# Linear attention with ReLU features: pairs of octets per load, six input buffers, K's copies in halves

## The chip, the cores and the metric

The kernel runs on one core of a Trainium2 chip. The metric is the device time of one execution in microseconds (us); a kernel's time is the median of several runs. A profile comes from one execution of its own.

## The reference

Q, K and V are fp32 arrays of 8 x 12 x 512 x 64 (batch, heads, sequence, dimension), drawn from a normal distribution.

```python
Q_feat = np.maximum(0, Q)
K_feat = np.maximum(0, K)
KV = np.einsum('bhkd,bhkv->bhdv', K_feat, V)
K_sum = np.sum(K_feat, axis=2)
numerator = np.einsum('bhqd,bhdv->bhqv', Q_feat, KV)
denominator = np.einsum('bhqd,bhd->bhq', Q_feat, K_sum)
return numerator / (denominator[:, :, :, None] + 1e-10)
```

Each of the 96 heads is independent. 36 MiB are read and 12 MiB written.

## The kernel before

**Tiling.** The 96 heads are taken in 12 octets of eight heads. An octet of one input is 1 MiB of fp32 that lies in one piece in memory; it is seen as 128 partitions of 8 KB (2048 numbers), so sixteen partitions hold one head. The loads are issued on POOL's queue (lines 176 to 187) and write bf16, 4 KB per partition, so the transfer casts. Only K and V of octet 0 are loaded otherwise: as fp32, from SP's queue, into two output buffers (line 264). There are seven buffers (`NI`) for each of Q, K and V, each a tile of its own, and ten output buffers of fp32 (`NOUT`).

**Waits and queues.** `Order` (line 9) works out which semaphores each instruction has to wait for, from the keys that instructions read and write; the program's order is written out by hand. Every load on POOL takes one of six lanes (semaphores gl0 to gl5) in turn and waits until the lane's load before it has landed, so at most six loads are under way. POOL issues its loads in program order: K, Q, V of octet 1, of octet 2 and so on. Before the first of them POOL clears and fills three small tiles: `ident` (line 268), the ones beside V in `vo` (lines 273 to 275) and `mask` (line 276).

**A step.** `step(i)` (line 311) does the first part of octet i and the last part of octet i - 1. PE transposes Q (line 363), ACT applies the ReLU (line 210), PE multiplies K by V in two halves of 16 products (line 372; half 0 waits for `a0` and `d0`, half 1 for `d1`), ACT copies the result out (line 218). Then the next octet is prepared: `prep_v` on ACT and DVE (lines 201 and 203), `copy_q` (line 207) and `prep_k` (line 192) on DVE. `prep_k` applies the ReLU and the mask and writes `kf`, once for each of two masks; for the octets of `HALVED` (2 to 8) each of the two copies is made in two halves, so that the first may start when PE has read half 0 of `kf`; for the others each is one instruction. DVE then normalises octet i - 1 (line 243, into `o_sb`), PE makes the denominators and the products with Q (line 357) and ACT copies these (line 226) for PE's transposes of the next step (line 381).

**Loads and stores in the steps.** Seven octets are loaded ahead of the steps; step i then loads octet i + 7, into the buffer of octet i. Stores go out on SP (line 252). Each store waits for its two normalised halves and, by a key that it reads, for K of the last octet to have landed: so no store moves before nearly all loads are through. In step 5, when all loads are issued, SP's program gets the stores of octets 0 to 3, then those of 4 and on.

Of the kernel before, what the change touches and what calls it, by code (L numbers as in the profile page):

```python
# [96 lines left out]
def kernel(  # L97
# [8 lines left out]
    B, H, S, D = Q.shape  # L106
    assert D == 64
    P = 128
    D1 = D + 1
    D4 = D + 4  # L110
    NH = B * H
    R = S * 4 // P
    RQ = S * 8 // P
    U = RQ // 2
    NO = NH // 8
    assert NO * 8 == NH and R == 16 and RQ == 32
    NI = 7
    NOUT = 10
    LANES = 6


    HALVED = range(2, 9)

    fp32 = mybir.dt.float32
    bf16 = mybir.dt.bfloat16
# [3 lines left out]
    sb = ctx.enter_context(tc.tile_pool(name="sb", bufs=1))  # L129
    psum = ctx.enter_context(tc.tile_pool(name="psum", bufs=1, space=bass.MemoryType.PSUM))  # L130

    def view(X, f):
        return X.rearrange("b h s d -> (b h s d)").rearrange("(n p f) -> n p f", p=P, f=f)

    Qr, Kr, Vr, Or = [view(X, RQ * D) for X in (Q, K, V, out)]

    ident = sb.tile([P, P], bf16, name="ident")
# [7 lines left out]
    q2 = sb.tile([P, U, P], bf16, name="q2")  # L145
# [2 lines left out]
    own = sb.tile([P, U, 8, 2], fp32, name="own")  # L148
    den = sb.tile([P, RQ], fp32, name="den")
    rec = sb.tile([P, RQ], fp32, name="rec")  # L150
    q_sb = [sb.tile([P, U, P], bf16, name=f"q_sb{i}") for i in range(NI)]
    k_sb = [sb.tile([P, RQ * D], bf16, name=f"k_sb{i}") for i in range(NI)]
    v_sb = [sb.tile([P, RQ * D], bf16, name=f"v_sb{i}") for i in range(NI)]
    o_sb = [sb.tile([P, RQ, D], fp32, name=f"o_sb{i}") for i in range(NOUT)]
    ps_kv = psum.tile([P, 2, 512], fp32, name="ps_kv")
    ps_den = ps_kv[:, 1, 256:512]
# [8 lines left out]
    def lane(who):  # L165
        turn[who] += 1
        return lanes[who][(turn[who] - 1) % len(lanes[who])]

    do = Order(nc, sems)

    def kv_src(o):
        if o == 0:
            return (o_sb[0], ("o", 0)), (o_sb[1], ("o", 1))
        return [(x[o % NI].rearrange("p (r d) -> p r d", d=D), (n, o % NI)) for n, x in (("k", k_sb), ("v", v_sb))]

    def load_q(o):
        do.op("pool", lambda e: e.dma_start(out=q_sb[o % NI].rearrange("p u f -> p (u f)"), in_=Qr[o],  # L177
                                            single_packet=True),
              writes=[("q", o % NI)], dma=lane("pool"))

    def load(o):
        i = o % NI
        for n, X, t in (("K", Kr, k_sb), ("V", Vr, v_sb)):
            if n == "V":
                load_q(o)
            do.op("pool", lambda e: e.dma_start(out=t[i], in_=X[o], single_packet=True), writes=[(n.lower(), i)],  # L186
                  dma=lane("pool"))

    def prep_k(o, s, halves=(0, 1)):
        src, key = kv_src(o)[0]  # L190
        rs = slice(R * halves[0], R * halves[-1] + R)
        do.op("dve", lambda e: e.tensor_scalar(kf[:, rs, s, :], src[:, rs], scalar1=0.0, scalar2=mask[:, 0, s:s + 1],  # L192
                                               op0=Alu.max, op1=Alu.mult),
              reads=[key, ("mask", 0)], writes=[("kf", s, j) for j in halves])
# [9 lines left out]
        do.op(who, make, reads=[key, ("mask", 1), "vo1"], writes=[("vo", t, j) for j in halves], sem=sem)  # L204

    def copy_q(o):
        do.op("dve", lambda e: e.tensor_copy(q2, q_sb[o % NI]), reads=[("q", o % NI)], writes=["q2"], sem="q2")  # L207

    def relu_q(j):
        do.op("act", lambda e: e.activation(qt[:, j * (U // 2):(j + 1) * (U // 2)], ps_qt[j], Act.Relu),  # L210
              reads=[("pq", j)], writes=[("qt", j)])
# [35 lines left out]
    def store(o):  # L247
        i = (o + 2) % NOUT
        to, src = Or[o], o_sb[i].rearrange("p r d -> p (r d)")
        keys = [("o", i, h) for h in range(2)]  # L250
        keys.append(("k", (NO - 1) % NI))
        do.op("sp", lambda e: e.dma_start(out=to, in_=src), reads=keys,
              dma=lane("sp" if o + NOUT < NO else "last"), kept=o + NOUT >= NO)
# [6 lines left out]
    def memset(who, ap, value, key):  # L260
        do.op(who, lambda e: e.memset(ap, value), writes=[key] if isinstance(key, (str, tuple)) else key)

    def body():
        for c, X in enumerate((Kr, Vr)):
            do.op("sp", lambda e: e.dma_start(out=o_sb[c].rearrange("p r d -> p (r d)"), in_=X[0]),  # L265
                  writes=[("o", c)], dma=lane("sp"))
        load_q(0)
        memset("pool", ident, 0.0, "ident")
        do.op("pool", lambda e: e.affine_select(out=ident, in_=ident, compare_op=Alu.not_equal, fill=1.0, base=0,
                                                pattern=[[-1, P]], channel_multiplier=1),  # L270
              reads=["ident"], writes=["ident"])
        ones = vo[:, :, :, 1:D4 - 1]
        memset("pool", ones[:, :, :, 0:D + 2:D1], 0.0, "vo1")
        for h in range(4):
            memset("pool", ones[32 * h:32 * h + 32, :, h % 2, 0:D + 2:D1], 1.0, "vo1")
        for h in range(4):
            for t in range(2):
                memset("pool", mask[32 * h:32 * h + 32, 1, t:t + 1], 1.0 if h % 2 == t else 0.0,
                       [("m", h, t), ("mask", 1)])
        for o in range(1, NI + 1):  # L280
            load(o)
            if o == 1:
                setup()
        for o in range(NO + 1):
            step(o)
        for n in lanes["pool"] + lanes["sp"]:
            nc.gpsimd.wait_ge(sems[n], do.count[n])
        nc.gpsimd.drain()

    def setup():  # L290
        do.op("dve", lambda e: e.tensor_copy(ident32, ident), reads=["ident"], writes=["ident32"])
        for c in range(2):
            do.op("dve", lambda e: e.tensor_reduce(
                out=mask_h[:, :, c], in_=ident32.rearrange("p (h b) -> p h b", h=8), op=Alu.add,
                axis=mybir.AxisListType.X), reads=["ident32"], writes=[("mh", c), "mask_h"])
        do.op("dve", lambda e: e.tensor_reduce(
            out=mask[:, 0, :], in_=mask_h[:, :, 0].rearrange("p (a s) -> p s a", s=2), op=Alu.add,
            axis=mybir.AxisListType.X), reads=["mask_h"], writes=[("mask", 0)])
        prep_k(0, 0)
        prep_k(0, 1)  # L300
        prep_v(0, 1, (0,), "act", "a0")
        prep_v(0, 0, (0, 1), "dve", "d0")
        prep_v(0, 1, (1,), "dve", "d1")
        do.op("dve", lambda e: e.memset(kvf.bitcast(fp32)[:, 0:4 * D1], 0.0), writes=KVD, sem="n0")
        do.op("dve", lambda e: e.memset(kvf.bitcast(fp32)[:, 4 * D1:], 0.0), writes=KVD, sem="n1")
        copy_q(0)
        for j in range(2):
            nc.scalar.sem_inc(sems[f"t{j}"], 1)
            do.note("act", "act", (), (), f"t{j}", 1)

    def step(i):
        r = i + 1
        more, last = i + 1 < NO, i == NO

        if not last:
            do.looped([("q2", r)], ["q2", "ident"], [("pq", 0)])
            do.looped([], ["q2", "ident"], [("pq", 1)])
            relu_q(0)
            relu_q(1)
            do.looped([("a0", r), ("d0", r)], KF[0], PK + ["pd"])  # L320
            do.looped([("d1", r)], KF[1], PK + ["pd"])
            evac_kv()
            if more:
                prep_v(i + 1, 1, (0,), "act", "a0")
                copy_q(i + 1)
                for halves in ((0,), (1,)) if i + 1 in HALVED else ((0, 1),):
                    prep_k(i + 1, 0, halves)
                    prep_k(i + 1, 1, halves)
        if i > 0:
            o = i - 1  # L330
            do.looped([("t0", r), ("t1", r)], [*OT, "ident32"], [("x", 0)])
            do.looped([], [*OT, "ident32"], [("x", 1)])
            for j in range(2):
                norm(o, j)
            if o + NI + 1 < NO:
                load(o + NI + 1)
            elif o + NI + 1 == NO:
                for x in range(o):
                    store(x)
            if o + NI + 1 >= NO:  # L340
                store(o)
        if not last:
            do.looped([("ev", r)], [*QT, *KVD], ["pd"])
            denominators()
            for j in range(2):
                do.looped([(f"n{j}", r)], [*QT, *KVD], [("x", j)])
            copy_ot(0, "act")
            copy_ot(1, "act" if more else "dve")
            if more:
                prep_v(i + 1, 0, (0, 1), "dve", "d0")  # L350
                prep_v(i + 1, 1, (1,), "dve", "d1")
# [48 lines left out]
    with tc.tile_critical(no_gpsimd_drain=True):  # L400
        body()
        products()
# [34 lines left out]
```

## Time and profile before

| | |
|---|---|
| median of 3 runs | 125.51 us (125.38 to 125.52) |
| profiled execution, its own time | 125.45 us |
| its span, first to last instruction | 123.7 us |
| PE, DVE, ACT, POOL busy | 69%, 69%, 63%, 20% |
| mean granted TensorE clock | 0.942 of full speed |
| read and written in HBM | 37.75 MB and 12.58 MB, 407 GB/s over the span |
| issues: loads on POOL, on SP; stores on SP | 34, 2; 12 |

The span is cut into 40 slices of 3.09 us in the page's table; a digit is the busy share of an engine in tenths. "DMA" is the share of the core's 16 DMA engines. A timeline line gives the start and the length in us, the engine, the line of the kernel, the operation, what it writes and reads, and in brackets the idle time before it and what ended it. A line on waits gives who waited for whom, the total in us, how often, and the longest. A line on one group's instructions gives least, median and largest duration in ns, then first and last start in us.

### The profile page before, as it was taken

The numbers are of one execution on the slowest core, as the hardware profiler recorded it, in microseconds if no ns is written. First come the engines' busy times: TensorE is split into PE (matmuls) and PEld (weight loads), VectorE is DVE, ScalarE is ACT, GpSimd is POOL, SyncE is SP. The second block draws the span as 40 slices with busy tenths as digits, with TensorE's granted clock in tenths as the row PEclk, the third lists the DMA queues.
The fourth block names the chain that finished last, engine by engine and source line by source line (L and its number), as shares of the span: only waits on it lengthen the run. The fifth ranks groups of instructions, "written<-read, shape, count | busy, mean of one in ns | idle before, by whom it ended". The sixth has DMA issues, their size and how long they took to land.

```text
span 123.7 us, 3418 instructions
## 1 busy us (share of the span) xinstructions
PE 85.0 (69%) x1440; PEld 73.7 (60%) x1440; DVE 84.9 (69%) x141; ACT 78.5 (63%) x108; POOL 24.9 (20%) x53
## 2 busy tenths in 40 slices
PE   0000098699797997979899797987969879655000
PEld 0000087699595986959689595876948759464000
DVE  1252921759989899898989989599595981937000
ACT  0000752996888989888998888889878888300000
POOL 5794111331131213212321131200000000000000
PEclk9999999859999999999999999999999999967855
DMA  2999999999999999999999999999999999999991
GB/s 58 391 315 236 212 215 217 216 212 213 213 213 212 212 213 212 212 216 215 212 212 215 220 212 212 215 215 212 212 307 423 424 427 427 424 429 432 427 427 42
DMA packets 6916, 32.55 MB, mean 263 GB/s; under 512 B 768, under 2 KB 768, under 8 KB 5120
## 3 DMA queue, kind: packets, MB, share of 16 engines
q0 software_dynamic: 4896, 17.83, 71.8%
q1 hardware_dynamic: 2016, 14.68, 28.7%
q14 instruction: 3, 0.02, 0.0%
q8 instruction: 1, 0.02, 0.0%
HBM read 37.75 MB, written 12.58 MB: 407 GB/s over the span
## 4 chain that ended last, share of the span: by engine, by line
PE 49%; DVE 30%; DMA 9%; issue 3%; ACT 1%; SPq 0%; DVEq 0%
DVE o_sb L243 22%; PE ps_kv L372 22%; PE ps_qt L363 11%; PE ps_x L381 10%; DMA o_sb<-in_V_dram 9%; PE ps_x L357 6%; DVE kf L192 3%; DVE vo L203 2%; ACT kvd L218 1%; DVE ot_sb L226 1%; PE ps_kv L357 0%; DVE q L207 0%; DVE den L235 0%; SPq L265 0%; DVE rec L238 0%
## 5 line engine op out<-in xcount | busy, mean ns | idle before, releaser
L243 DVE TENSOR_TENSOR o_sb<-ps_x,rec 128x1024 f32<-128x1024 f32 x24 | 28.5, 1220 | 6.5 <-PE ps_x L381 5.5
L372 PE MATMUL ps_kv<-vo,kf 64*128 64x132 bf16 x768 | 27.0, 230 | 0.6
L226 ACT COPY ot_sb<-ps_x 128x1024 f32<-128x1024 f32 x23 | 23.2, 1013 | 5.9 <-PE ps_x L357 4.9
L372 PEld LDWEIGHTS ps_kv<-vo,kf 64*128 64x128 bf16 x768 | 25.2, 100 | 2.4 <-issue 2.4
L381 PE MATMUL ps_x<-ident,ot_sb 128*128 128x128 f32 x192 | 25.2, 288 | 1.7 <-DVE ot_sb L226 1.7
L363 PE MATMUL ps_qt<-ident,q 128*128 128x128 bf16 x192 | 14.3, 234 | 16.8 <-DVE q L207 15.7
L192 DVE TENSOR_SCALAR kf<-k_sb,mask 128x1024 bf16<-128x1024 bf16 (+1 forms) x36 | 18.0, 542 | 9.9 <-PE ps_kv L372 9.5
L210 ACT ACTIVATE qt<-ps_qt 128x1024 bf16<-128x1024 bf16 x24 | 23.4, 1030 | 1.9 <-PE ps_qt L363 1.9
L381 PEld LDWEIGHTS ps_x<-ident,ot_sb 128*128 128x128 f32 x192 | 22.3, 148 | 3.2 <-issue 2.0
L363 PEld LDWEIGHTS ps_qt<-ident,q 128*128 128x128 bf16 x192 | 12.2, 106 | 19.5 <-DVE q L207 15.7
L218 ACT CAST kvd<-ps_kv 64x260 bf16<-64x260 f32 x48 | 18.0, 374 | 8.6 <-PE ps_kv L372 7.8
L357 PE MATMUL ps_x<-qt,kvd 128*128 128x256 bf16 x96 | 14.5, 275 | 7.3 <-DVE o_sb L243 7.0
L357 PEld LDWEIGHTS ps_x<-qt,kvd 128*128 128x128 bf16 x96 | 7.6, 98 | 12.0 <-DVE o_sb L243 10.5
L201 ACT ACTIVATE vo<-v_sb,mask 128x1024 bf16<-128x1024 bf16 x11 | 12.7, 1154 | 0.3
L203 DVE TENSOR_SCALAR vo<-v_sb,mask 128x2048 bf16<-128x2048 bf16 (+1 forms) x22 | 11.6, 569 | 0.0
L177 POOL DMA_DIRECT2D q_sb<-in_Q_dram x12 | 7.6, 630 | 18.2 <-DMA q_sb<-in_Q_dram 15.2
L186 POOL DMA_DIRECT2D v_sb<-in_V_dram x11 | 7.1, 650 | 18.3 <-DMA v_sb<-in_V_dram 17.0
L186 POOL DMA_DIRECT2D k_sb<-in_K_dram x11 | 6.8, 622 | 16.9 <-DMA k_sb<-in_K_dram 16.9
L207 DVE COPY q<-q_sb 128x2048 bf16<-128x2048 bf16 x12 | 8.2, 683 | 2.4 <-PE ps_qt L363 2.4
L201 ACT ACT_TABLE_LOAD x1 | 1.3, 1283 | 12.5 <-DMA o_sb<-in_V_dram 12.5
L357 PE MATMUL ps_kv<-kvd,qt 128*128 128x16 bf16 x192 | 6.9, 179 | 1.7 <-ACT kvd L218 1.7
L357 PEld LDWEIGHTS ps_kv<-kvd,qt 128*128 128x128 bf16 x192 | 6.5, 96 | 1.9 <-ACT kvd L218 1.8
(20 smaller groups left out, 26.5 us busy)
## 6 DMA issues: line engine op xcount, KB each, us to landing
out_dram<-o_sb SPq DMA_DIRECT2D x12, 1024.0 KB, 14.4
q_sb<-in_Q_dram POOLq DMA_DIRECT2D x12, 512.0 KB, 14.5
k_sb<-in_K_dram POOLq DMA_DIRECT2D x11, 512.0 KB, 14.4
v_sb<-in_V_dram POOLq DMA_DIRECT2D x11, 512.0 KB, 14.5
o_sb<-in_K_dram SPq DMA_DIRECT2D x1, 1024.0 KB, 6.5
o_sb<-in_V_dram SPq DMA_DIRECT2D x1, 1024.0 KB, 11.0
```

The lines of the kernel that those rows point to most:

```text
L186: do.op("pool", lambda e: e.dma_start(out=t[i], in_=X[o], single_packet=True), writes=[(n.lower(), i)], dma=lane("pool"))
L192: do.op("dve", lambda e: e.tensor_scalar(kf[:, rs, s, :], src[:, rs], scalar1=0.0, scalar2=mask[:, 0, s:s + 1], op0=Alu.max, op1=Alu.mult) ...
L201: make = lambda e: e.activation(to, src, Act.Copy, scale=m)
L203: make = lambda e: e.tensor_scalar(to, src, scalar1=m, scalar2=None, op0=Alu.mult)
L210: do.op("act", lambda e: e.activation(qt[:, j * (U // 2):(j + 1) * (U // 2)], ps_qt[j], Act.Relu), reads=[("pq", j)], writes=[("qt", j)])
L218: do.op("act", lambda e: e.copy(kvd[64 * c:64 * c + 64, s:8:2, c * D1:c * D1 + D1].rearrange("p (g t) d -> p g t d", t=2), ps_kv[64 * s:64 ...
L226: do.op(who, lambda e: e.copy(to, src) if who == "act" else e.tensor_copy(to, src), reads=[("x", j)], writes=[("ot", j)], sem=f"t{j}")
L243: do.op("dve", lambda e: e.tensor_tensor(o_sb[i][:, rs], ps_x[j].rearrange("p (r d) -> p r d", d=D), rec[:, rs].unsqueeze(2).to_broadcast( ...
L357: return pe.matmul(out_, lhsT, rhs, start=True, stop=True, skip_group_check=True)
L363: x = pe.transpose(ps_qt[u // 8][:, u % 8, :], q2[:, u, :], ident)
L372: x = pe.matmul(ps_kv[:, h, 0:2 * (D + 2)].rearrange("p (t d) -> p t d", t=2), kf[ps, R * g + k, :, :].rearrange("p s d -> p (s d)"), vo[p ...
L381: x = pe.transpose(ps_x[u // 8][:, u % 8 * P:u % 8 * P + P], ot[:, u].rearrange("p h c -> p (h c)"), ident32)
```

## The change

Three things are changed, and one at POOL's start.

- **Loads.** Octet 1 is loaded as before, K, Q, V, each for itself. From octet 2 on, the octets are loaded in pairs: one transfer for Q of both, one for K of both, then V of each. Octets 2 to 5 are loaded ahead of the steps; steps 1, 3 and 5 load the pairs 6/7, 8/9 and 10/11.
- **Buffers.** Six instead of seven for each input; the six lie side by side in one tile, so that a pair's transfer writes two neighbours.
- **K's copies.** `HALVED` is gone: `prep_k` is made in halves for all octets from 1 on.
- **POOL's start.** `ident` is cleared in four pieces of 32 columns; the ones' places in `vo` are cleared in four pieces of eight rows, and the ones are written in eight pieces, not four.

```diff
-    NI = 7
+    NI = 6
...
-    HALVED = range(2, 9)
...
-    q_sb = [sb.tile([P, U, P], bf16, name=f"q_sb{i}") for i in range(NI)]
-    k_sb = [sb.tile([P, RQ * D], bf16, name=f"k_sb{i}") for i in range(NI)]
-    v_sb = [sb.tile([P, RQ * D], bf16, name=f"v_sb{i}") for i in range(NI)]
+    ins = {n: sb.tile([P, NI, RQ * D], bf16, name=f"{n}_sb") for n in "qkv"}
...
-    def load(o):
-        i = o % NI
-        for n, X, t in (("K", Kr, k_sb), ("V", Vr, v_sb)):
-            if n == "V":
-                load_q(o)
-            do.op("pool", lambda e: e.dma_start(out=t[i], in_=X[o], single_packet=True), writes=[(n.lower(), i)],
-                  dma=lane("pool"))
+    def load(n, *octets):
+        o, i, m = octets[0], octets[0] % NI, len(octets)
+        src = {"q": Qr, "k": Kr, "v": Vr}[n][o:o + m].rearrange("n p f -> p n f")
+        do.op("pool", lambda e: e.dma_start(out=ins[n][:, i:i + m], in_=src, single_packet=True),
+              writes=[(n, x % NI) for x in octets], dma=lane("pool"))
+
+    def load_two(o):
+        load("q", o, o + 1)
+        load("k", o, o + 1)
+        load("v", o)
+        load("v", o + 1)
...
-        load_q(0)
-        memset("pool", ident, 0.0, "ident")
+        load("q", 0)
+        for c in range(4):
+            memset("pool", ident[:, 32 * c:32 * c + 32], 0.0, [("i", c), "ident"])
...
-        memset("pool", ones[:, :, :, 0:D + 2:D1], 0.0, "vo1")
+        for c in range(4):
+            memset("pool", ones[:, 8 * c:8 * c + 8, :, 0:D + 2:D1], 0.0, "vo1")
         for h in range(4):
-            memset("pool", ones[32 * h:32 * h + 32, :, h % 2, 0:D + 2:D1], 1.0, "vo1")
+            for j in range(2):
+                memset("pool", ones[32 * h:32 * h + 32, R * j:R * j + R, h % 2, 0:D + 2:D1], 1.0, "vo1")
...
-        for o in range(1, NI + 1):
-            load(o)
-            if o == 1:
-                setup()
+        for n in "kqv":
+            load(n, 1)
+        setup()
+        load_two(2)
+        load_two(4)
...
-                for halves in ((0,), (1,)) if i + 1 in HALVED else ((0, 1),):
-                    prep_k(i + 1, 0, halves)
-                    prep_k(i + 1, 1, halves)
+                for j in range(2):
+                    prep_k(i + 1, 0, (j,))
+                    prep_k(i + 1, 1, (j,))
...
-            if o + NI + 1 < NO:
-                load(o + NI + 1)
-            elif o + NI + 1 == NO:
-                for x in range(o):
-                    store(x)
-            if o + NI + 1 >= NO:
+            if i % 2 and i + 6 < NO:
+                load_two(i + 5)
+                if i + 7 == NO:
+                    for x in range(o):
+                        store(x)
+            if i + 7 >= NO:
                 store(o)
```

More of the change, by code (lines that the diff above doesn't have):

```diff
@@ L173, in kv_src @@
             return (o_sb[0], ("o", 0)), (o_sb[1], ("o", 1))
[L174 to L179, printed above, removed]
-    def load(o):
-        i = o % NI
-        for n, X, t in (("K", Kr, k_sb), ("V", Vr, v_sb)):
-            if n == "V":
-                load_q(o)
-            do.op("pool", lambda e: e.dma_start(out=t[i], in_=X[o], single_packet=True), writes=[(n.lower(), i)],
-                  dma=lane("pool"))
+        return [(ins[n][:, o % NI].rearrange("p (r d) -> p r d", d=D), (n, o % NI)) for n in "kv"]
+    def load(n, *octets):
[8 more added lines that the diff above has]
+        load("v", o + 1)
     def prep_k(o, s, halves=(0, 1)):
@@ L206, in copy_q @@
     def copy_q(o):
-        do.op("dve", lambda e: e.tensor_copy(q2, q_sb[o % NI]), reads=[("q", o % NI)], writes=["q2"], sem="q2")
+        do.op("dve", lambda e: e.tensor_copy(q2.rearrange("p u f -> p (u f)"), ins["q"][:, o % NI]),
+              reads=[("q", o % NI)], writes=["q2"], sem="q2")
     def relu_q(j):
```

## The prediction

> **What bounds the kernel now.** I read the 40 slices first, then the DMA queues, then what SP's queue and POOL waited for, then the timeline. The slices:
>
> ```profile
> DVE  1252921759989899898989989599595981937000
> DMA  2999999999999999999999999999999999999991
> GB/s 58 391 315 236 212 215 217 216 212 213 213 213 212 212 213 212 212 216 215 212 212 215 220 212 212 215 215 212 212 307 423 424 427 427 424 429 432 427 427 42
> ...
> q0 software_dynamic: 4896, 17.83, 71.8%
> q1 hardware_dynamic: 2016, 14.68, 28.7%
> ```
>
> The DMA engines are full from the second slice to the last but one, while DVE stops three slices (9 us) before the end. The loads look half as fast as the stores only because the row counts the bf16 that is written: 214 GB/s of it is 428 GB/s of fp32 read, the stores' rate. Now POOL's issues and SP's last wait:
>
> ```profile
> 29.28 0.53 POOL L186 DMA_DIRECT2D k_sb<-in_K_dram  x1 [1.93 <-DMA k_sb<-in_K_dram]
> ...
> 78.43 0.75 POOL L186 DMA_DIRECT2D v_sb<-in_V_dram  x1 [1.93 <-DMA v_sb<-in_V_dram]
> ...
> SPq L408 <- DMA out_dram<-o_sb: 7.5, 1, 7.5
> ```
>
> From the first of these issues to the second there are 20 steps: (78.43 - 29.28) / 20 = 2.4575 us per transfer of 1 MiB read. Each issue waits only for a lane (the transfer six before), so POOL follows the DMA and does not lead it. At the end SP waits 7.5 us for stores that were issued long before. The chain of waits names PE (49%) and DVE (30%), because it walks back from the last store's issue; but the last normalisation is over at 114.3 us and the span at 123.7:
>
> ```profile
> 113.08 1.23 DVE L243 TENSOR_TENSOR o_sb<-ps_x,rec 128x1024 f32<-128x1024 f32 x1 [0.35 <-PE ps_x L381]
> ...
> 120.00:121.00 1.00, 0.00 (x0) 0.00 (x0) 0.00 (x0) 0.00 (x0) 0.00 (x0) 0.50 0.76 320
> 121.00:122.00 1.00, 0.00 (x0) 0.00 (x0) 0.00 (x0) 0.00 (x0) 0.00 (x0) 0.50 0.14 57
> ```
>
> So the end is set by 48 MiB of transfers at 2.45 us each behind a start. The compute has slack: the last store moves for 2.45 us before its landing near 122.7 us, so its turn comes at 120.2; SP's first transfer was issued at 0.96 and moved data within about 1 us; it could be issued near 119 instead of 114.3, a **slack of some 4.7 us**. The two windows show one more thing: the DMA share falls to 0.14 before it is nil. One DMA engine runs behind the rest (landing records of the last store: 121.05 us on the first engine, 122.69 on the last; the same lag of 1.3 us is there from the load of K1 on). That late engine sets the end, and the others have over 1 us to spare.
>
> **Part 1, fewer transfers.** POOL issues 34 loads now (Q 12, K 11, V 11). After the change: Q0, three for octet 1, and per pair of octets Q, K, V, V, five times: 4 + 20 = 24, **ten fewer**, with the same bytes. What does one transfer cost beside its bytes? In the trace's packet records every transfer ends on each engine with one 4-byte packet of 22 ns (the page counts 768 packets under 512 B: 48 transfers by 16 engines), and data packets start 304.5 ns apart: 8 x 304.5 + 21.5 = 2457.5 ns, which is the whole pace above. So a removed transfer is worth 21.5 ns, ten of them **-0.21 us**, straight on the end, as the engines never idle. Bounds: nothing if those packets hide; at most what the best 1-us slice of the stores (437 GB/s, 2.40 us per MiB) leaves of the pace, 0.058 us, ten times: -0.58 us. I take -0.21, the measured packet.
>
> **Part 2, geometry of the pairs.** Each descriptor still reads 8 KB and writes 4 KB, but an engine now alternates between two octets 1 MiB apart. 20 MiB move so, 20 x 2.4575 = 49.15 us. The trace has no such transfer; nearest are today's loads and the stores, 2.4575 and about 2.45 us per MiB though one casts and the other doesn't, so I take no change. Each per cent of loss would be +0.49 us; a gain is bounded by Part 1's 437 GB/s, 20 x 0.058 = -1.2 us, and I see no reason for it.
> The Trainium skill (DMA: Bandwidth & Descriptors, Latency and other measured facts) reports that copies whose rows lie 512 KiB, 2 MiB or 4 MiB apart fall from about 214 to 207, 164 and 103 GB/s. No transfer of this trace has such rows; by its 2 MiB figure the sum would be 49.15 x (214/164 - 1), an estimate of 15 us more. Against it: here only two rows stand 1 MiB apart, and the 128 partitions lie side by side.
>
> **Part 3, the order of the loads.** Octet 1 keeps K, Q, V. After V1 (landed at 19.2 us) come Q of 2 and 3, K of 2 and 3, V2, V3: K2 lands after 4 MiB, 19.2 + 4 x 2.45 = 29.0 us (now 21.7), V2 at 31.4 (now 26.5). The users now:
>
> ```profile
> 27.74 1.83 DVE L192 TENSOR_SCALAR kf<-k_sb,mask 128x1024 bf16<-128x1024 bf16 x4 [1.14 <-PE ps_kv L372]
> ...
> 30.28 1.16 ACT L201 ACTIVATE vo<-v_sb,mask 128x1024 bf16<-128x1024 bf16 x1
> ```
>
> K2's copies start 29.0 - 27.7 = 1.2 us late, ACT's V copy 1.1 us late beside them. Queued behind on DVE: both normalisations of octet 0, so the n semaphores, PE's products and the ACT copies: the whole compute slips by 1.2 us. It doesn't grow: a pair of octets loads in 6 x 8 x 0.3045 + 4 x 0.0215 = 14.7 us, and two steps take 47.57 - 32.82 = 14.75 us (first Q transposes of steps 2 and 4), so later pairs arrive just as the slipped steps need them. V10 lands near 90.2 for an ACT copy now at 89.60, which the slip covers. All this lies in the 4.7 us of slack: **0**. Without that cover it would be +1.2 us.
>
> Lanes: a load still waits for the one six before it, and with doubles among these at least 7 MiB, 17 us of work, are in flight. Six buffers: the pair 6/7 overwrites octet 1's after step 0, which ends some 20 us before the lane frees at V2's landing or later. Stores: K of 10 and 11 is again followed by 2 MiB (V10, V11, before Q11, V11), so SP's twelve stores, gated on K11, go at the same place, 0.2 us earlier.
>
> **Part 4, K's copies in halves for octets 1, 9, 10, 11.** A step with whole copies is longer now: 77.09, 84.77, 92.58, 100.42 are the Q transposes of steps 8 to 11, periods 7.68, 7.81, 7.84 against 7.38: -0.30 - 0.43 - 0.46 = -1.2 us for compute, about what Part 3 costs it. DVE spends 1.83 instead of 1.42 us on four pieces, inside PE's product. Compute ends near 114.3 again; on the path: **0**. If loads didn't bound the end, both would count.
>
> **Part 5, POOL's start.** The clearing of ident goes from 1 to 4 pieces, vo's from 1 to 4, vo's ones from 4 to 8: ten more instructions ahead of K1's issue.
>
> ```profile
> L261 POOL MEMSET mask<- x8: 89/92/94, 5.0 to 6.0; 32x1 f32 x8
> L261 POOL MEMSET vo<- x5: 371/372/529, 2.7 to 4.5; 32x64 bf16 x4, 128x128 bf16 x1
> L261 POOL MEMSET ident<- x1: 224/224/224, 2.1 to 2.1; 128x128 bf16 x1
> ...
> 6.04 0.55 POOL L186 DMA_DIRECT2D k_sb<-in_K_dram  x1
> ...
> 7.63 1.38 POOL L186 DMA_DIRECT2D k_sb<-in_K_dram  x1
> 8.99 1.20 POOL L177 DMA_DIRECT2D q_sb<-in_Q_dram  x1
> ```
>
> One element costs 92 ns, and starts lie about 0.05 us further apart than durations. Ten more such floors are 10 x 0.14 = **+1.4 us** (0 if pieces only share the old time; if each cost its old whole, 3 x 0.27 + 3 x 0.58 + 4 x 0.42 = +4.2), so K1 is issued at 7.4 instead of 6.0 (10.3 at worst). There it meets DVE's fp32 copies of K0 (7.59 to 10.07), during which the two last rows took 1.38 and 1.20 us instead of 0.53: K1's issue ends near 8.8, and with SP's 1 us to first data it is ready at 9.8. The engines need it when K0, V0 and Q0, 3 MiB or 7.4 us from 2.7 on, are through: 10.1, and 11.3 on the late engine. **0**, with 1.5 us to spare where it counts.
> The Trainium skill (SBUF — State Buffer, Who interferes with whom) says why those rows are long: a tensor_scalar copy in a 2-port mode holds the ports that GpSimd shares, and the other side blocks fully. The trace agrees: 1.38 against 0.53.
>
> **Sum**: 125.45 (profiled execution; span 123.7 and 1.75 around it) - 0.21 = 125.24. The median of the runs is 0.06 higher than that execution, so **125.3**. About 0.2% (0.25 us) is what a measurement here can tell from no change; the forecast lies just inside it.
>
> **Rivals.**
> *K1 comes too late* (slower). Place: the start, Part 5. It decides once K1 is ready later than 11.3 us on the late engine, that is memsets dearer by over 2.9 us in place of 1.4. At worst: issued 10.3, done 10.8, data 11.8, hence +0.5 on the late engine, -0.21: 125.8; with a second slow issue behind it 126.0. For: ten more floors, DVE's hold. Against: the small instructions are cheap by their rows. 0.13.
> *Pairs move slower* (slower). Part 2 at 1%: +0.49 - 0.21 = 125.8; slower than before by 0.2% from 0.9% on. For: never seen here. Against: two different kinds of transfer keep one pace. 0.08. The row-pitch rule of the Trainium skill, cited under Part 2, speaks for this rival.
> *Compute becomes the bound.* It needs a slip over 4.7 us where 1.2 - 1.2 is expected; a slip repeated in each of the five pairs would be 6.0 - 1.2 = 4.8, +0.1 - 0.21 at most: 125.3 to 125.4, and 125.9 if each slip were 1.3. 0.04.
> *It saves nothing*, the small packets being covered, or a small loss eating the gain: 125.5. For: 22 ns is close to what two packets overlap (324 long, 304.5 apart). 0.12.
> *More is saved*: Part 1's upper bound, 124.9. Against: the packet records leave no other gap. 0.05.
>
> **How the numbers follow.** The forecast has 0.58, with its own range 125.0 to 125.45; 0.36 of it lies under 125.26. Faster 0.36 + 0.05 = 0.41; within 0.2% 0.22 + 0.12 = 0.34; slower 0.13 + 0.08 + 0.04 = 0.25. The range, 124.9 to 126.0, goes from Part 1's upper bound to the late K1.
>
> **What would show it.** Right: 608 packets under 512 B instead of 768; the DMA row full as before; POOL's K1 issue near 7.4 us; DVE's K copy of octet 2 waiting for a DMA until about 29.0; last normalisation near 114.3, SP's last wait about 7.3 us. Wrong: a DMA slice under 9 near 10 us (K1), load slices below 210 GB/s (pairs), or SP's last wait gone (compute).

## The result, and the profile after

The changed kernel takes 126.15 us in the median of 13 runs (125.62 to 126.95). The kernel before, run beside it, takes 125.39 (125.24 to 125.72, 13 runs). The ratio is 1.006, with a 95% interval of 1.0038 to 1.0082: **slower by 0.6%**. The forecast was 125.3, and the range ended at 126.0. The profiled execution of after took 125.79 us, 0.34 more than that of before; its span is 124.0 against 123.7. This profile thus shows less than half of the loss of 0.76 us between the medians; longer runs of after are profiled under the experiments. All ratios here are of fast runs; the only slow ones are four of the twelve of `e13_less_late`, its profiled run among them.

The slices of after's page:

```profile
DVE  0354725624976989989898998989899895596100
...
PEclk9999999999559999999999999999999999999755
DMA  2999999999999999999999999999999999999991
GB/s 61 403 311 217 201 209 217 211 215 214 214 214 211 211 217 215 211 215 217 213 215 211 214 215 214 213 215 214 215 312 422 420 426 428 423 426 431 434 412 42
DMA packets 6756, 32.55 MB, mean 263 GB/s; under 512 B 608, under 2 KB 608, under 8 KB 4960
```

The small packets are 608, as ten transfers fewer should make them. From the seventh slice to the last load the rate is that of before. Only slices 4, 5 and 6 are lower: 217, 201, 209 where before had 236, 212, 215. The DMA row hides it: it shows a 9 in those slices too. POOL's start in after's timeline (start, length, engine, line, operation):

```profile
2.12 0.69 POOL L256 MEMSET ident<- 128x32 bf16 x4
...
3.12 3.29 POOL L256 MEMSET vo<- 128x32 bf16 x12
6.46 1.13 POOL L256 MEMSET mask<- 32x1 f32 x8
7.54 1.32 POOL L174 DMA_DIRECT2D k_sb<-in_K_dram  x1
8.85 1.20 POOL L174 DMA_DIRECT2D q_sb<-in_Q_dram  x1
10.04 0.54 POOL L174 DMA_DIRECT2D v_sb<-in_V_dram  x1
```

K1 is issued at 7.54 us, where before issued it at 6.04. The fills of `vo` now take 3.29 us instead of 2.25, those of `ident` 0.69 instead of 0.22. What the DMA engines did in two of the next microseconds; the last three columns are clock, DMA share and GB/s. After:

```profile
10.00:11.00 1.00, 0.00 (x0) 0.00 (x0) 0.00 (x0) 0.00 (x0) 1.00 (x3) 1.00 0.97 160
...
13.00:14.00 1.00, 0.00 (x0) 0.00 (x0) 1.00 (x3) 0.99 (x2) 0.20 (x1) 1.00 0.93 188
```

And before:

```profile
10.00:11.00 1.00, 0.00 (x0) 0.00 (x0) 0.07 (x1) 0.00 (x0) 0.19 (x1) 1.00 1.06 217
...
13.00:14.00 1.00, 0.00 (x0) 0.00 (x0) 1.00 (x2) 0.99 (x2) 0.00 (x0) 1.00 1.16 233
```

When K0, V0 and Q0 are through, the engines find too little queued: 160 GB/s instead of 217, and 188 instead of 233 three microseconds later. At 214 GB/s the first is (217 - 160) / 214 = 0.27 us of work lost, and the second, against a steady 214, (214 - 188) / 214 = 0.12 us: together 0.39 us. The packet records show it too: between 8 and 20 us before has no data packet that takes over 0.5 us, while after has ten, of 0.54 to 0.69 us, all starting between 10.12 and 10.48 us. They lie on the loads' queue and are probably the first of K1; the records do not name the transfer.

The landing records have 16 times for each transfer, one for each DMA engine. The span ends 0.99 us behind the last of them, before and after. They give a balance for the late engine, which sets the end:

| us | before | after | difference |
|---|---|---|---|
| V of octet 1 landed | 19.16 | 19.64 | +0.48 |
| from there to V of octet 11 landed | 75.07 | 74.86 | -0.21 |
| from there to the last store landed | 28.46 | 28.48 | +0.02 |
| last store landed | 122.69 | 122.98 | +0.29 |

So, in this profile, **the loss is all made before 20 us**, and the ten saved transfers are there, at the predicted size, between. The lag of the late engine differs from run to run; the mean of the 16 landings is steadier. V of octet 1 landed at 18.04 us in the mean before and at 18.40 after, +0.36, close to the 0.39 of the two windows; from there to the last store the mean takes 103.37 us before and 103.22 after, -0.15. The compute is later too; three lines of after's timeline, and what SP waited for at the end:

```profile
29.58 1.74 DVE L186 TENSOR_SCALAR kf<-k_sb,mask 128x1024 bf16<-128x1024 bf16 x4 [3.92 <-DMA k_sb<-in_K_dram]
...
31.95 1.16 ACT L195 ACTIVATE vo<-v_sb,mask 128x1024 bf16<-128x1024 bf16 x1 [3.40 <-DMA v_sb<-in_V_dram]
...
112.75 2.36 DVE L238 TENSOR_TENSOR o_sb<-ps_x,rec 128x1024 f32<-128x1024 f32 x2 [1.32 <-PE ps_x L380]
```

```profile
SPq L407 <- DMA out_dram<-o_sb: 7.0, 1, 7.0
```

DVE waits 3.92 us for K2 (the two 5s of the clock row are behind this wait), and the last normalisation ends at 115.1 instead of 114.3. SP still waits 7.0 us after that for stores, so these 0.8 us cost nothing.

### The profile page after: what moved, and what is told of

The parts are those of the page before. It is cut to its first block, busy times and chain, and to the rows that moved or that the text cites. A ratio compares the mean times of both kernels' runs of the same rounds, so it can differ in the third digit from the quotient of the medians.

```text
span 124.0 us, 3416 instructions
## 1 busy us (share of the span) xinstructions
PE 84.2 (68%) x1440; PEld 72.5 (58%) x1440; DVE 86.2 (70%) x149; ACT 78.3 (63%) x108; POOL 22.1 (18%) x53
## 3 DMA queue, kind: packets, MB, share of 16 engines
q0 software_dynamic: 4736, 17.83, 71.7%
## 4 chain that ended last, share of the span: by engine, by line
PE 43%; DVE 24%; DMA 15%; POOL 7%; issue 4%; POOLq 0%; DVEq 0%; SPq 0%
DVE o_sb L238 21%; PE ps_kv L371 17%; DMA k_sb<-in_K_dram 15%; PE ps_x L380 11%; PE ps_qt L362 9%; PE ps_x L356 5%; POOL vo L256 2%; POOL q_sb L174 2%; DVE kf L186 1%; POOL k_sb L174 1%; DVE ot_sb L221 1%; PE ps_kv L356 1%; POOL mask L256 1%; POOL v_sb L174 0%; POOL ident L256 0%
## 5 line engine op out<-in xcount | busy, mean ns | idle before, releaser
L186 DVE TENSOR_SCALAR kf<-k_sb,mask 128x1024 bf16<-128x1024 bf16 x44 | 19.4, 485 | 9.8 <-PE ps_kv L371 5.3
L380 PE MATMUL ps_x<-ident,ot_sb 128*128 128x128 f32 x192 | 23.6, 276 | 1.7 <-DVE ot_sb L221 1.7
L380 PEld LDWEIGHTS ps_x<-ident,ot_sb 128*128 128x128 f32 x192 | 20.8, 140 | 3.2 <-issue 2.0
L356 PE MATMUL ps_x<-qt,kvd 128*128 128x256 bf16 x96 | 15.3, 287 | 9.2 <-DVE o_sb L238 8.8
L195 ACT ACTIVATE vo<-v_sb,mask 128x1024 bf16<-128x1024 bf16 x11 | 12.7, 1154 | 3.6 <-DMA v_sb<-in_V_dram 3.4
L174 POOL DMA_DIRECT2D q_sb<-in_Q_dram x7 | 5.4, 771 | 9.1 <-DMA v_sb<-in_V_dram 5.8
L174 POOL DMA_DIRECT2D k_sb<-in_K_dram x6 | 4.9, 821 | 6.8 <-DMA v_sb<-in_V_dram 5.1
```

Of the source, the lines that this page charges most:

```text
L174: do.op("pool", lambda e: e.dma_start(out=ins[n][:, i:i + m], in_=src, single_packet=True), writes=[(n, x % NI) for x in octets], dma=lane ...
L195: make = lambda e: e.activation(to, src, Act.Copy, scale=m)
L356: return pe.matmul(out_, lhsT, rhs, start=True, stop=True, skip_group_check=True)
L380: x = pe.transpose(ps_x[u // 8][:, u % 8 * P:u % 8 * P + P], ot[:, u].rearrange("p h c -> p (h c)"), ident32)
```

## The experiments

Theory: POOL's longer start issues octet 1's loads late, and the engines run short of work near 10 us. Rivals: the pairs themselves are slower; DVE's fp32 copies of K0, which share the time from 7.5 to 10 us with the issues, hold them up; the compute sets the end in the longer runs; the way in which the fills are split does the harm, not the time they take. Where an expectation uses a short name, A2 is the theory of DVE's copies, F the fetch of code that the first runs brought up, and G a fixed time of 3 to 4 us from POOL's issue to data. All the kernels compute the whole reference. The runs at a glance, each ratio against the kernel before on the same chip:

| run | K1 issued at | GB/s, 10 to 11 us | median us | ratio, 95% interval |
|---|---|---|---|---|
| e1_old_fills | 6.02 | 217 | 125.82 | 1.0023 (1.0013 to 1.0033) |
| e2_new_fills_alone | 7.55 | 152 | 125.99 | 1.0045 (1.0027 to 1.0063) |
| e3_loads_first | 2.10 | 213 | 125.46 | 0.9997 (0.9989 to 1.0006) |
| e4_after_again | 7.54 | 180 | 126.53 | 1.0068 (1.0046 to 1.0090) |
| e5_pad_after | 6.02 | 221 | 125.35 | 0.9996 (0.9987 to 1.0004) |
| e6_before_loads_first | 2.12 | 217 | 125.39 | 1.0001 (0.9992 to 1.0009) |
| e8_pad_ahead | 6.47 | 217 | 125.33 | 0.9991 (0.9982 to 0.9999) |
| e9_late_by_pads | 7.69 | 148 | 125.97 | 1.0049 (1.0029 to 1.0070) |
| e10_k1_first | 2.12; Q1 at 10.11 | 225 | 126.28 | 1.0070 (1.0051 to 1.0088) |
| e11_k0_on_act | 7.55 | 107 | 125.90 | 1.0045 (1.0027 to 1.0063) |
| e12_later_still | 11.46 | 41 | 128.75 | 1.0275 (1.0254 to 1.0297) |
| e13_less_late (spoiled) | 6.84 | 205 | 126.21 | 1.0051 (1.0027 to 1.0075) |
| e14_octets_2_3_single | 7.54 | 148 | 125.72 | 1.0026 (1.0014 to 1.0037) |
| e16_pad_and_single | 6.48 | 225 | 125.47 | 0.9996 (0.9987 to 1.0004) |
| e18_less_late_clean | 6.85 | 217 | 125.44 | 0.9998 (0.9989 to 1.0007) |
| e19_early_k0_on_act | 6.48 | 209 | 125.37 | 0.9994 (0.9985 to 1.0004) |

**The fills alone, and the loads alone.** `e1_old_fills` is after with POOL's old fills; `e2_new_fills_alone` is before with the new ones. Both differ from their base by these lines:

```diff
-        for c in range(4):
-            memset("pool", ident[:, 32 * c:32 * c + 32], 0.0, [("i", c), "ident"])
+        memset("pool", ident, 0.0, "ident")
...
-        for c in range(4):
-            memset("pool", ones[:, 8 * c:8 * c + 8, :, 0:D + 2:D1], 0.0, "vo1")
+        memset("pool", ones[:, :, :, 0:D + 2:D1], 0.0, "vo1")
         for h in range(4):
-            for j in range(2):
-                memset("pool", ones[32 * h:32 * h + 32, R * j:R * j + R, h % 2, 0:D + 2:D1], 1.0, "vo1")
+            memset("pool", ones[32 * h:32 * h + 32, :, h % 2, 0:D + 2:D1], 1.0, "vo1")
```

> The changed kernel with POOL's fills of ident and vo in the old few pieces, so that K1 of octet 1 is issued near 6.0 us again; pairs, six buffers and halves stay. Theory A (K1, and with it Q1, is issued too late, the DMA engines run dry near 10 us): the loss goes and the saved packets show, 125.2 us, ratio to before 0.998, little spread. Theory B (transfers of two octets are slower): as the changed kernel, about 126.1. Theory C (the compute, held up by the later K2, becomes the bound in the longer runs): about 126.1 with its spread of over 1 us.

> The kernel before with the new fills alone (ten more instructions on POOL ahead of K1); loads, buffers and copies as before. Theory A: slower by the whole loss, 0.76 plus the 0.21 that the pairs save, some 126.3 us, with the wide spread of the changed kernel. Theories B and C: 125.4, as before.

e2, with no pair in it, is slower by 0.45%, at 125.99 us where the theory asked for 126.3: the fills alone bring a loss, and the same low window:

```profile
10.00:11.00 1.00, 0.00 (x0) 0.00 (x0) 0.02 (x1) 0.00 (x0) 1.00 (x3) 1.00 0.89 152
```

e1 has K1 at 6.02 us and no low window, and yet it was 0.2% slower than before, where 0.2% faster was expected. Its last store landed at 122.66 us, no later than before's 122.69, but its span is 124.1. What lies behind the last store is a small transfer in the last microsecond:

```profile
121.00:122.00 1.00, 0.00 (x0) 0.00 (x0) 0.00 (x0) 0.00 (x0) 0.00 (x0) 0.50 0.10 41
122.00:123.00 1.00, 0.00 (x0) 0.00 (x0) 0.00 (x0) 0.00 (x0) 0.00 (x0) 0.50 0.00 0
123.00:124.00 1.00, 0.00 (x0) 0.00 (x0) 0.00 (x0) 0.00 (x0) 0.00 (x0) 0.50 0.03 8
```

The packet records name it: 8 KB on q14, the queue of instructions, at 123.997 us. In after the last such packet comes at 72.5 us, in before at 79.4. e1's POOL program is ten instructions shorter than either of these: before has ten more loads, after ten more fills.

**The same loads, issued early.** `e3_loads_first` keeps the new fills and puts octet 1's loads ahead of them; `e4_after_again` is after itself in the same batch.

```diff
         load("q", 0)
+        for n in "kqv":
+            load(n, 1)
         for c in range(4):
...
-        for n in "kqv":
-            load(n, 1)
         setup()
```

> The changed kernel with K, Q and V of octet 1 issued right behind Q of octet 0, ahead of all fills, which keep their new pieces. Theory A: no dry engines at 10 us, 125.2 us, faster than before by 0.2%. Theories B and C: about 126.1.

> The changed kernel once more on this chip, for a second profile and its spread beside the others: about 126.1 us, runs from 125.6 to 127. Theory A: in a longer run the DMA share between 10 and 18 us is lower and the landing of V1 later by what the run is longer. Theory C: V1 lands as in the first profile, and SP's last wait for the stores is gone.

e3 has no low window:

```profile
10.00:11.00 1.00, 0.00 (x0) 0.00 (x0) 0.05 (x1) 0.00 (x0) 0.63 (x7) 1.00 1.04 213
```

It takes 125.46 against 126.53 for after beside it: **moving three issues takes the whole loss away**, with all the pairs and all the fills still there. V1 lands at 18.99. The expected gain of 0.2% did not come: the kernel is as fast as before.

**The length of the program.** `e5_pad_after` is e1 with ten tiny fills of a spare tile behind the loads that are issued ahead of the steps; `e8_pad_ahead` has them ahead of K1. `e6_before_loads_first` is before with octet 1's loads ahead of the fills.

```diff
+    spare = sb.tile([P, 16], fp32, name="spare")
...
+        for c in range(10):
+            memset("pool", spare[0:32, c:c + 1], 0.0, ("spare", c))
```

> The run with the old fills, and ten tiny fills of a spare tile on POOL behind its ahead-of-time loads (near 30 us, where POOL waits anyway), so that POOL's program is as long as the changed kernel's. In the run with the old fills the last landing was at 122.66 us, yet an 8 KB code fetch began at 123.997 and the span ended at 124.1. Theory F (its 0.33 us over the kernel before is that code fetch behind the last wait, which a longer program moves forward): no fetch after 120 us, 125.45. Theory B (the transfers of two octets cost it): 125.8 as without the ten.

> The same ten tiny fills with the old fills, but ahead of K1's issue, which they move from 6.0 to about 7.4 us, as in the changed kernel; program as long as there. Theory A (only the lateness counts, not what POOL does meanwhile): 126.2 with a spread of over 0.7 us, DMA rate between 10 and 11 us down to 150 to 180 GB/s from 217. Else, if the split fills themselves cost it: 125.5.

> The kernel before (single octets, seven buffers, old fills) with K, Q, V of octet 1 issued ahead of the fills, the counterpart of the changed kernel with its loads first (125.46). Theory A as it stands (the engines never run dry here, before or after): 125.45, as before. If the pairs cost time that the early issue hides in their run: 125.2 here.

e5 is back at 125.35, with no packet of code behind 72.7 us. Ten useless instructions made e1 faster by 125.82 - 125.35 = 0.47 us between the medians. In the profiles the span ends 1.41 us behind the last store's landing in e1 and 0.99 us in e5, as in before and after: 0.42 us of it is the fetch. e8 missed its expectation: ten such fills, which wait for nothing, cost only 0.39 us together, so K1 was hardly late:

```profile
6.13 0.39 POOL L257 MEMSET spare<- 32x1 f32 x10
6.47 0.55 POOL L175 DMA_DIRECT2D k_sb<-in_K_dram  x1
```

So e8 is one more kernel with pairs and early loads, at 125.33. e6 shows that loads earlier than before's 6.04 us bring nothing.

**Late by other means.** `e9_late_by_pads` has the old fills and ten dearer ones ahead of K1, each of which waits for the one before; `e12_later_still` has twenty. In `e10_k1_first` only K1 goes ahead of the new fills, Q1 and V1 stay behind. In `e11_k0_on_act` ACT makes the two copies of K0, so DVE is idle while POOL issues.

```diff
+    spare = sb.tile([P, 16], bf16, name="spare")
...
+        for c in range(10):
+            memset("pool", spare, 0.0, ["spare", ("mask", 1)])
         for n in "kqv":
             load(n, 1)
```

```diff
-        prep_k(0, 0)
-        prep_k(0, 1)
+        for s in range(2):
+            src, key = kv_src(0)[0]
+            do.op("act", lambda e: e.activation(kf[:, :, s, :], src, Act.Relu, scale=mask[:, 0, s:s + 1]),
+                  reads=[key, ("mask", 0)], writes=[("kf", s, j) for j in range(2)])
```

> Old fills, and ahead of K1's issue ten dearer fills of a spare tile (16 columns, each waiting for the one before), which move the issue to about 7.5 us; the ten tiny ones of the run before had moved it to 6.47 only, at no loss. Theory A (lateness alone): 126.2 with a wide spread, a dip of the DMA rate at 10 to 11 us. If the split fills themselves are the cause: 125.35.

> The changed kernel with K1 alone issued ahead of the fills, Q1 and V1 where they were. Theory A in its narrow form (the engines run dry once, when Q0 and V0 are through and K1 is not there): 125.5. If the second dip of the changed kernel near 13 us (188 and 156 GB/s in its two profiles) is a lateness of Q1 by itself: 125.8 to 126.0, with that dip and without the one at 10 us.

> The changed kernel, with the two copies of K0 made on ACT in place of DVE (ACT waits for V0 at that time anyway): K1 is still issued at 7.5 us, but DVE makes no fp32 copy beside it. Theory A1 (the issue alone is late): K1's packets still miss 10.1 us by little, 125.8 or more. Theory A2 (the issue is late and meets DVE's copies, which stretch POOL's issues and what stands behind them): issues of 0.55 us in place of 1.3 and 1.2, V1 out by 9.2 us, no dips, 125.35.

> As the run with ten dear fills ahead of K1, with twenty: K1 is issued at about 9.3 us instead of 7.69. Where the DMA rate came back in the late runs, K1's data flowed 3.1 to 3.9 us behind the start of its issue. Theory G (from POOL's issue to data 3 to 4 us at this place, whatever DVE does): data flow again at 12.4 to 13.2 us, the late engine loses 1.1 to 1.9 us: 126.4 to 127.2. Theory A as first priced (issue 1.3 us and 1 us to data): data at 11.6, a loss of 0.3 on the late engine, 125.6 to 125.8.

e9, whose fills are the old ones, is as slow as e2: the time counts, not the way the fills are split. In e10 the eight fills of `mask`, which fell beside DVE's copies of K0, took 3.17 us instead of 1.13, and Q1 was issued at 10.11. The loss, 0.7% at 126.28 us, is larger than the 125.8 to 126.0 that was expected, and the low windows moved with the late issue:

```profile
12.00:13.00 1.00, 0.00 (x0) 0.00 (x0) 0.51 (x1) 0.53 (x1) 1.00 (x2) 1.00 0.87 172
13.00:14.00 1.00, 0.00 (x0) 0.00 (x0) 1.00 (x2) 0.99 (x2) 0.90 (x1) 1.00 0.79 156
```

In e12 the twenty fills, among which the same copies fell, took 5.41 us, so K1 was not issued at 9.3 us as expected, but at 11.46:

```profile
6.12 5.41 POOL L257 MEMSET spare<- 128x16 bf16 x20
11.46 0.55 POOL L175 DMA_DIRECT2D k_sb<-in_K_dram  x1
```

```profile
11.00:12.00 1.00, 0.00 (x0) 0.00 (x0) 0.00 (x0) 0.00 (x0) 0.83 (x5) 1.00 0.04 16
12.00:13.00 1.00, 0.00 (x0) 0.00 (x0) 0.81 (x1) 0.83 (x1) 1.00 (x3) 1.00 0.60 41
13.00:14.00 1.00, 0.00 (x0) 0.00 (x0) 1.00 (x2) 0.99 (x2) 1.00 (x2) 1.00 0.60 98
```

Here the engines stand idle, which measures what the prediction had to borrow from SP: the ten first packets of K1 that the records have were taken up at 12.7 to 12.8 us, took 0.6 to 1.1 us each, and data flowed at the usual 0.32 us a packet from 13.7. That is **2.2 us from the start of POOL's issue and 1.7 from its end**, not 1.0, and, with idle engines, not the 3 to 4 us that one theory held. The run took 128.75 us, more than either theory had expected, as the issue came two microseconds later than planned.

In e11 DVE is idle, K1's issue takes 0.55 us instead of 1.32, and V1 is out at 9.17; still the rate fell, to 107 GB/s from 10 to 11 us and 111 in the next. DVE's copies are not the cause. The first long packets start at 9.84 us here, 1.7 behind the issue's end, but they take 1.1 to 2.0 us, and the first to end do so at 11.3, 3.2 us behind it.

**How late is late, and ACT's part.** `e13_less_late` has five dear fills ahead of K1 and five behind the loads that are issued ahead of the steps. `e18_less_late_clean` is the same without a fault that e13's trace showed. `e19_early_k0_on_act` is e8 with e11's copies on ACT.

```diff
         load_two(4)
         for c in range(5):
-            memset("pool", spare, 0.0, ["spare", ("mask", 1)])
+            memset("pool", spare, 0.0, "spare")
```

> The same with five of the ten fills ahead of K1, the other five behind the ahead-of-time loads (the program is as long): K1 issued at about 6.9 us. Theory G: data at 10.0 to 10.8 against a need at 10.1 (11.3 on the late engine): 125.35 to 125.5, nearly nothing lost. If any K1 issue within DVE's copies of K0 (from 7.5 us on) is what counts, none is here but V1's: 125.35.

> e13_less_late again without the fault that its trace shows: there the five fills behind the loads counted as writers of mask, so that ACT's and DVE's copies of V1 waited 8.5 us for them (until 30.90) and the compute, not the loads, set the end. Here they write a spare tile alone. K1 is issued near 6.84 us, Q1 near 7.4 (1.5 us long), V1 near 8.9. If the wait made all of e13's loss: 125.35 to 125.5, 205 GB/s or more from 10 to 11 us. If 0.4 us of lateness beyond e8_pad_ahead's 6.47 already leaves the engines short: 125.6 to 125.9, and the late engine lands V1 after 19.3 us.

> e8_pad_ahead (K1 issued at 6.47) with the two copies of K0 on ACT. It tells whether the long dip of e11_k0_on_act (107 GB/s from 10 to 11 us) came from the late issue or from ACT's copies at 7.5 to 11 us. If from the late issue alone: no dip, 205 GB/s or more from 10 to 11 us, 125.3 to 125.5. If from ACT's copies: the dip is there although K1 is early, 125.6 to 126.0.

e13 missed, and it was the experiment that was wrong. Its second five fills counted as writers of `mask`, so the copies of V1 waited for POOL to get past the loads; the list of waits says so:

```profile
ACT vo L196 <- POOL spare L257: 8.5, 1, 8.5
```

That is over the 4.7 us of slack, and in its profile the last normalisation ended at 120.9 us and SP waited only 3.0 us after it: the compute was the bound. It tells nothing of K1. e18, without the wait, has K1 at 6.85 us and 125.44, and the rate holds:

```profile
10.00:11.00 1.00, 0.00 (x0) 0.00 (x0) 0.17 (x1) 0.00 (x0) 1.00 (x2) 1.00 1.06 217
```

So **0.8 us later than before costs nothing, 1.5 us costs between 0.26% (e14, below) and 0.7%**. In e19 ACT makes the same copies as in e11, with K1 at 6.48, and the rate holds. The same window in e11:

```profile
10.00:11.00 1.00, 0.00 (x0) 0.00 (x0) 0.00 (x0) 1.00 (x2) 0.59 (x1) 1.00 1.40 107
```

And in e19:

```profile
10.00:11.00 1.00, 0.00 (x0) 0.00 (x0) 0.00 (x0) 1.00 (x2) 0.00 (x0) 1.00 1.03 209
```

So there, too, the lateness does it; why the rate fell lowest with the shortest issues stays open.

**Why some runs are longer.** After's runs go from 125.5 to 127.0 us, before's only from 125.1 to 125.7. `e14_octets_2_3_single` is after with octets 2 and 3 loaded one by one, K1 as late; `e16_pad_and_single` is the same edit to e8; `e15_after_look` and `e17_after_look_two` are after again, one profile each.

```diff
-        load_two(2)
+        for o in (2, 3):
+            for n in "kqv":
+                load(n, o)
         load_two(4)
```

> The changed kernel with octets 2 and 3 loaded one by one (K, Q, V each), pairs from octet 4 on; the fills and the late K1 stay. DVE and PE then don't wait for K2 near 28 us. If the long runs of the changed kernel (126.4 to 127) come from the compute, which falls behind at half clock after that wait and ends too late for the last store: the long runs go, all between 125.5 and 126.1, median 125.8. If they come from the late DMA engine alone: spread and median as the changed kernel, 126.2 with runs to 126.9.

> The changed kernel, one look. The late engine's theory: the landing of V1 tells the run's length (19.64 us for 125.79, 19.97 for 126.34). The compute's theory: in a run over 126.5 the last normalisation ends after 118 us and SP's last wait is under 6 us.

> Early K1 (old fills, ten tiny ones, 125.33 us) with octets 2 and 3 one by one. The compute isn't held up, two packets more than in that run: 125.3 to 125.4, runs within 0.3 us of each other, last normalisation before 113.5 us.

> The changed kernel, a second look. As for the first look: the late engine's theory reads the length from V1's landing, the compute's theory from the end of the last normalisation.

Four profiles of after by the mean landing of V1 over the 16 engines (its last landing in brackets): 18.32 (19.01) in the run of 125.71, 18.40 (19.64) in that of 125.79, 18.83 (19.97) in that of 126.34, 19.15 (20.66) in that of 126.53. Before has 18.04 (19.16). So the last engine alone does not tell a late start, as e17's 19.01 lies ahead of before's 19.16; the mean does. In the longest of the four (e15) K1 was issued at 7.56, as always, but the engines moved only 107 GB/s from 10 to 11 us, where the first profile of after had 160; the compute ended near 116.0, and SP still waited 6.9 us for stores (6.3 in e4). The longer runs are those in which the engines fall further behind at the start, not those in which the compute does.

All the profiles agree with this balance. The mean landing of V1 lies between 17.94 and 18.14 us in every run that issues both K1 and Q1 before 7.5 us, and between 18.32 and 21.20 in every other. From there to the last store the mean takes 103.37 or 103.38 us in the three kernels without pairs (before, e2, e6) and 103.16 to 103.24 in those with all pairs, whether early or late; only e13 falls out, where the compute holds up the stores. e14 and e16, with two more transfers, have 103.31 and 103.22.

e14 taken alone came out as the theory of the compute had it: 11 of 12 runs lie between 125.62 and 125.92, and the ratio is 1.0026. The long waits for stores in e4 and e15 speak against that theory. Part of the loss may come with pairs issued right behind a late start, but that is not shown: e2, without any pair, has runs of 126.42 and 126.53 among its eight. What sets how far the engines fall behind is not settled. Where K1 is early, the same edit brings nothing (e16).

## Why the prediction was wrong

**The step that failed** is in Part 5: "K1's issue ends near 8.8, and with SP's 1 us to first data it is ready at 9.8." The issue itself was priced well: predicted at 7.4 and ending near 8.8, measured 7.54 and 8.86. The time to data was not. By e12's 1.7 us from the issue's end, K1 is ready at 8.86 + 1.7 = 10.5, not 9.8, and 0.4 us after the 10.1 at which the prediction saw the engines run dry; the windows showed 0.39 us lost. A latency of POOL's path had been read from a row of SP's, and that row was read too short: its 1 us runs from the start of SP's issue (0.96 us) to the first packets (1.99), but it was added to the end of POOL's issue, and it stops at the first packets. From the end of SP's issue (1.35) to the 2.7 us from which the prediction itself counts the flow are 1.35 us, which would have made K1 ready at 8.8 + 1.35 = 10.15. Nor is the time one fixed number: e11 would have been ready by it at 8.10 + 1.7 = 9.8 and ran short, with 3.2 us to the end of its first long packets. So the agreement of 0.4 with 0.39 may be luck; that the time was taken too short is shown, what sets it stays open.

**"With 1.5 us to spare where it counts"** failed too. The late engine was taken to have 1.2 us in hand, because it comes to K1 later. It kept its lag instead: V1's first engine was 0.25 us later than before (18.08 against 17.83), its last 0.48. In e12 the late engine did use up its lag, which was 0.52 us at V1 instead of 1.33; but at the last store it was 1.64 again, as in before, and first and last engine both landed 2.88 us later. So lag on the engine that sets the end was no cover for a shortage that hits all engines; why it comes back is not shown. The Trainium skill (DMA: Bandwidth & Descriptors, Latency and other measured facts) reports that two of the engines are usually slower in traces; the lag of one engine agrees (V1 of before landed at 19.16 us on it and by 18.11 on the others), though no record here numbers it.

**The rival** "K1 comes too late" had the place and the mechanism right and was priced at 125.8 to 126.0. Its condition was wrong: it asked for fills dearer by 2.9 us, and 1.5 were enough (e2, e9). Its chance of 0.13 rested on the same borrowed 1 us.

**Its own tests** would have misled. A DMA slice under 9 near 10 us was to show a late K1: the digits stayed at 9, as packets that take long count as busy. Load slices under 210 GB/s were to show slow pairs: 201 and 209 stand there, but in the slices of the late start, and e2 has a low window without any pair.

**Part 1** held: -0.21 us predicted, 74.86 - 75.07 = -0.21 on the late engine, and 0.13 to 0.21 less in the mean of the engines in every profile with all pairs but e13's. The total shows less of it. Leaving out e1 with its fetch, the six versions with pairs and an early start (e3, e5, e8, e16, e18, e19) have ratios of 0.9991 to 0.9998, mean 0.9995, some 0.06 us; only that of e8 has an interval clear of 1, and just so (0.9982 to 0.9999). In e3 the mean of the last store's landings is 0.19 us earlier than before (121.22 against 121.41), but the last of them is not (122.66 against 122.69): the late engine's lag took the gain. Part 1's upper bound was no bound: its 437 GB/s came from slices of 0.9 us, and in before single windows of 1 us reach 451 GB/s; the forecast did not use it, but the range's lower end did.

**Part 2** held: a pair of octets loads in 14.70 us, as six MiB in four transfers should. Rows of two octets 1 MiB apart show no loss. The rule on row pitch from the Trainium skill (DMA: Bandwidth & Descriptors, Latency and other measured facts) would have added 15 us by the estimate there; nothing of that is seen here, where only two octets lie so far apart and the partitions of each side by side.

**Parts 3 and 4**: K2's copies start 29.58 - 27.74 = 1.84 us later, 1.2 expected, the rest being V1's delay of 0.48 and a little more. One half-clock window of 3.4 us, which before has near 24 us, became two behind the wait. By the Trainium skill (TensorE: Matmul & The Clock Gate, Part 1) the clock is halved after an idle window of about 3.4 us. The trace agrees on the length (two windows of 3.41 us, 30.9 to 37.8), but not on the idleness: PE was busy for 1.70 us of the 3.4 us ahead of them, and in before for 1.74. The compute ended 0.8 us later, at 115.1 and not near 114.3 again as Part 4 has it, but inside the slack. Cost on the path: 0, as predicted; only e13's added 8.5 us broke through.

**The program's length** was left out. Ten loads fewer make POOL's program shorter, and e1 against e5 shows that it can cost 0.47 us; the ten added fills happened to make up for it, which was luck.

## What to carry to other kernels

Where the loads are the bound, work put ahead of the first issues of a queue can come onto the path, however small each piece; issue the loads first and fill the tiles behind them (e3), or measure how much start the engines really need: here 0.8 us more was free and 1.5 was not. The time from issue to data has to come from the same queue, and a lag of the engine that sets the end must not be counted as slack. A full DMA row does not say that engines have work: read the bytes moved in each microsecond beside it. And where one engine's lag wanders, compare the mean landing over all engines.

## What the runs showed of the hardware

- **A code fetch behind the last wait.** A POOL program shorter by ten instructions brought an 8 KB fetch at 123.997 us, 1.3 us after the last store had landed. The span ended 1.41 us behind that landing instead of 0.99, and the median was 0.47 us higher (e1 against e5).
- **POOL's fills.** Ten fills of 32x1 that wait for nothing take 0.39 us (e8); the eight of `mask`, of the same size, each behind the one before, take 1.13 (after). Ten of 128x16, each behind the one before, take 1.64 (e9), and twenty, with DVE's fp32 copies of K0 falling among them, take 5.41 (e12).
- **A short queue looks busy.** With 107 GB/s moved, the DMA share of that microsecond in e11 was 1.40: single packets took 1.1 to 2.0 us there, against 0.32 in the steady flow.
